# A streamed ReLU and row sum on one core: all loads but the first two blocks move to GpSimd's queue

## The chip, the core and the metric

The kernel runs on one core of one Trainium2 chip. The metric is the device time of one execution in microseconds (us), and smaller is better. A core has separate engines that run their own instruction streams and meet at semaphores: TensorE (PE, unused here), VectorE (DVE), ScalarE (ACT), GpSimd (POOL) and SyncE (SP). Data moves between HBM and the on-chip memory SBUF by 16 DMA engines, which take transfers from queues; an engine's instruction stream issues a transfer to a queue and goes on.

## The reference

```python
x = np.random.randn(32, 512, 1024).astype(np.float32)
relu_x = np.maximum(x, 0)
return np.sum(relu_x, axis=-1).astype(np.float32)
```

The input has 16,384 rows of 1,024 floats, 67.1 MB. Each row is clamped at zero and summed, which leaves 16,384 floats, 65.5 KB.

## The kernel before

The 16,384 rows are dealt out to the 128 partitions of SBUF, 128 rows to each, and worked on in eight blocks of 16 rows per partition. One block is [128 partitions, 16 rows, 1024 columns] of float32, 8.39 MB, and 64 KB in a row of SBUF. Three buffers, io0 to io2, are used in turn, so block j uses buffer j mod 3. The first block is a part of its own of the input; the other seven are cut from the rest. Either way the 16 rows of one partition lie next to each other in HBM, and a whole block moves as 128 packets of 65,536 bytes, eight on each of the 16 DMA engines.

The list `TWO` says how a block is computed. For the first three blocks ACT clamps the whole block in place (`clamp`, L120) and DVE then sums each row (`total`, L128). The fourth and fifth block do it in two halves, and the sixth in two parts of 7 rows with two further rows on ACT alone (`act_row`, L135, which clamps and sums one row). The seventh block is done row by row, nine rows by ACT and seven by DVE alone (`dve_row`, L143). The eighth block is the tail. It comes in shrinking loads of 8 rows, 4 rows, 2 rows and 280 columns, then the last row with the last 260 columns of the row before it, and at last two pieces of 240 and 244 columns of that row before it, which have small buffers of their own (piece0, piece1). Its rows are split between ACT and DVE too, and the last piece's sum is made on L227 from the piece and the partial sums beside it.

The helper `load` (L99) issues every load from SP, in order, on one hardware queue. Each load has its own semaphore, which reaches 16 when all 16 DMA engines have finished their share. From the fourth block on a load first waits on the semaphore `dve`, until DVE is done with the block that last used the buffer. Behind the 13 loads SP issues three stores (`store`, L110) of the row sums: the first block's 16 sums of each partition, then 110 sums, and the last 2. Then SP clears the semaphores (L46) and waits for the stores (L47).

`open_without_barrier` takes the opening barrier out and puts the first load (`EARLY = 1`) at the very start of SP's program. GpSimd does nothing but four small memsets of constants, which belong to the framework's opening. The order of all instructions is written out by hand; no scheduler moves them.

Of the kernel before, what the change touches and what calls it, by code (L numbers as in the profile page):

```python
# [9 lines left out]
ROWS = 16  # L10
NBUF = 3


TWO = [[16], [16], [16], [8, 8], [8, 8], [7, 7], []]
# [5 lines left out]
TAIL = [8, 4]  # L20
START_PIECE, END_PIECE = 280, 260
PIECES = [240, 244]

EARLY = 1


def kernel(tc: tile.TileContext, x: bass.AP, out: bass.AP):
    nc = tc.nc
    sems = Semaphores(tc)

    tc.close()
    tc.compile()
    nc.cur_bb = nc.bb_map[tc.start_bb_name]
    body = nc.cur_bb.bb.instructions
    ends = list(body)
    body.clear()
    n_stores = relu_sum(nc, sems, x, out)
    body.extend(ends)


    nc.cur_bb = nc.bb_map[tc.start_bb_name + "_end"]
    nc.cur_bb.bb.instructions.clear()
    nums = sorted(s.num for s in (*sems.loads, sems.act, sems.dve))
    cleared = range(nums[0], nums[-1] + 1)
    assert len(cleared) == len(nums)
    nc.sync.sem_clear(cleared)  # L46
    nc.sync.wait_ge(sems.stored, 16 * n_stores).then_inc(sems.stored, -16 * n_stores)  # L47
    open_without_barrier(tc, EARLY)


class Semaphores:
    def __init__(self, tc: tile.TileContext):
        n = len(TWO) + len(TAIL) + 2 + len(PIECES)
        self.loads = [tc.alloc_semaphore(f"load{i}") for i in range(n)]
        self.act = tc.alloc_semaphore("act")
        self.dve = tc.alloc_semaphore("dve")
        self.stored = tc.alloc_semaphore("stored")


def relu_sum(nc, sems: Semaphores, x: bass.AP, out: bass.AP):  # L60
# [24 lines left out]
    def rows(m, n):  # L85
        if m < ROWS:
            return xf[:, m : m + n, :]
        return xv[:, m - ROWS : m - ROWS + n, :]

    def sums(m, n):  # L90
        if m < ROWS:
            return of[:, m : m + n], res[:, m : m + n]
        return ov[:, m - ROWS : m - ROWS + n], res[:, m : m + n]

    n_load = n_act = n_dve = n_store = 0

    def load(dst, src, after=None):
        nonlocal n_load
        dma = nc.sync.dma_start(out=dst, in_=src)  # L99
        if after:  # L100
            dma.wait_op(sems.dve, after[1], "sem-ge")
        dma.then_inc(sems.loads[n_load], 16)
        n_load += 1
        return sems.loads[n_load - 1]

    def store(m, n, act, dve):
        nonlocal n_store
        dst, src = sums(m, n)
        nc.sync.wait_ge(sems.act, act)
        nc.sync.dma_start(out=dst, in_=src).wait_op(sems.dve, dve, "sem-ge").then_inc(  # L110
            sems.stored, 16
        )
        n_store += 1

    def clamp(ap, loaded):
        nonlocal n_act
        if n_act == 0:
            nc.scalar.preload_act_table(RELU).wait_op(loaded, 16, "sem-ge")  # L118
            loaded = None
        i = nc.scalar.activation(out=ap, in_=ap, func=RELU)  # L120
        if loaded is not None:
            i.wait_op(loaded, 16, "sem-ge")
        i.then_inc(sems.act, 1)
        n_act += 1

    def total(ap, m, n):
        nonlocal n_dve
        nc.vector.tensor_reduce(  # L128
            out=res[:, m : m + n], in_=ap, axis=mybir.AxisListType.X, op=ADD
        ).wait_op(sems.act, n_act, "sem-ge").then_inc(sems.dve, 1)  # L130
        n_dve += 1

    def act_row(ap, accum_out, loaded):
        nonlocal n_act
        i = nc.scalar.activation(out=ap, in_=ap, func=RELU, accum_out=accum_out)  # L135
        if loaded is not None:
            i.wait_op(loaded, 16, "sem-ge")
        i.then_inc(sems.act, 1)
        n_act += 1

    def dve_row(ap, accum_out, loaded):
        nonlocal n_dve
        i = nc.vector.tensor_scalar(  # L143
            out=ap,
            in0=ap,
            scalar1=0.0,
            scalar2=None,
            op0=MAX,
            op1=ADD,
            accum_out=accum_out,  # L150
        )
        if loaded is not None:
            i.wait_op(loaded, 16, "sem-ge")
        i.then_inc(sems.dve, 1)
        n_dve += 1

    freed = []
    m = 0
    for j in range(NB):
        buf = bufs[j % NBUF]  # L160
        loaded = load(buf[:, :, :], rows(m, ROWS), j >= NBUF and freed[j - NBUF])
        c = 0
        act_waits = dve_waits = loaded
        for n in TWO[j]:
            clamp(buf[:, c : c + n, :], act_waits)
            total(buf[:, c : c + n, :], m + c, n)
            act_waits = None
            c += n
        for _ in range(ACT[j]):
            act_row(buf[:, c, :], res[:, m + c : m + c + 1], act_waits)  # L170
            act_waits = None
            c += 1
        for _ in range(DVE[j]):
            dve_row(buf[:, c, :], res[:, m + c : m + c + 1], dve_waits)
            dve_waits = None
            c += 1
        assert c == ROWS
        freed.append((n_act, n_dve))
        m += ROWS


    buf = bufs[NB % NBUF]
    c = 0
    for n in TAIL:
        loaded = load(
            buf[:, c : c + n, :], rows(m, n), None if c else freed[NB - NBUF]
        )
        for i in range(n):
            if i % 2 == 0 or (n == 8 and i == 7):
                act_row(buf[:, c, :], res[:, m : m + 1], loaded if i == 0 else None)  # L190
            else:
                dve_row(buf[:, c, :], res[:, m : m + 1], loaded if i == 1 else None)
            c += 1
            m += 1

    flat = buf[:, :, :].rearrange("p c d -> p (c d)")
    src = rows(m, 4).rearrange("p c d -> p (c d)")
# [4 lines left out]
    last, w = parts[-1], PIECES[-1]  # L202
    others = [last[:, w + i : w + i + 1] for i in range(extra)]
    loaded = load(flat[:, at : at + b], src[:, :b])
    act_row(buf[:, c, :], res[:, m : m + 1], loaded)
    sums_act = n_act
# [3 lines left out]
    loaded = load(flat[:, at + end : at + 4 * D], src[:, end:])  # L210
# [13 lines left out]
    for i in range(len(PIECES) - 1):  # L224
# [3 lines left out]
        out=last[:, :],  # L228
# [6 lines left out]
    ).wait_op(sems.dve, n_dve, "sem-ge").then_inc(sems.dve, 1)  # L235
    n_dve += 1
    store(NT - 2, 2, n_act, n_dve)
    return n_store


def open_without_barrier(tc: tile.TileContext, n_loads: int):

    SP = mybir.EngineType.SP
    blocks = tc.nc.main_func.blocks
    opening = blocks[0].instructions
    body = next(b for b in blocks if b.name == tc.start_bb_name).instructions
    for i in list(opening):
        if isinstance(i, (mybir.InstDrain, mybir.InstEventSemaphore)):  # L250
            opening.remove(i)
    loads = [i for i in body if i.engine == SP][:n_loads]
    for i in loads:
        assert isinstance(i, mybir.InstDMACopy)
        body.remove(i)
    at = next(n for n, i in enumerate(opening) if i.engine == SP)
    opening[at:at] = loads
# [30 lines left out]
```

## Time and profile before

| what | value |
|---|---|
| time, median of 3 runs | 161.13 us (160.91 to 161.22) |
| span of the profiled execution, first to last instruction | 159.84 us |
| median time less that span (time around it) | 1.29 us |
| DVE busy | 117.6 us, 74% |
| ACT busy | 104.2 us, 65% |
| POOL busy | 0.2 us |
| DMA, mean over the span | 420 GB/s; packets take 97.9% of the 16 engines' span |
| HBM read | 67.11 MB |

The page gives an engine's busy time as a share of the span. A DMA packet is what one DMA engine moves at a stretch for one queue. "SPq" is the instruction stream of SP, which issues transfers and waits. A load's landing is the moment at which the last of its 16 semaphore increments arrives.

The trace also holds a start, a duration and a size for every packet, and the time of every semaphore increment. Where the text speaks of "the packet records" or "the landing records", it means these.

### The profile page before, as it was taken

How to read it: one execution, taken by the hardware profiler on the slowest of the kernel's cores; microseconds unless marked ns; L12 is line 12 of the kernel's file. 1: busy time of each engine (PE TensorE's matmuls, PEld its weight loads, DVE VectorE, ACT ScalarE, POOL GpSimd, SP SyncE). 2: the span in 40 equal slices, each digit the busy share in tenths (PEclk: the TensorE clock that was granted, in tenths of full speed). 3: DMA queues.
4: the chain of work that ended last, by engine and by line, in shares of the span. 5: the costliest groups of instructions: out<-in, count | busy, mean ns of one | idle time of the engine just before them, and what ended most of it. 6: DMA issues, size and time to landing. Idle time of an engine off the chain costs nothing.

```text
span 159.8 us, 120 instructions
## 1 busy us (share of the span) xinstructions
DVE 117.6 (74%) x43; ACT 104.2 (65%) x50; POOL 0.2 (0%) x4
## 2 busy tenths in 40 slices
DVE  0000000006999799994999999999999999999986
ACT  0000049993699808996099951999329993499994
POOL 0000000000000000000000000000000000000000
DMA  8996996996996997999989969969969969898993
GB/s 279 508 508 279 525 508 279 525 492 295 525 492 295 525 459 328 525 394 394 525 361 426 525 295 492 525 262 525 508 279 525 508 279 525 377 410 385 425 416 102
DMA packets 2304, 67.18 MB, mean 420 GB/s; under 512 B 640, under 2 KB 896, under 8 KB 1024
## 3 DMA queue, kind: packets, MB, share of 16 engines
q1 hardware_dynamic: 2304, 67.18, 97.9%
HBM read 67.11 MB, written 0.07 MB: 420 GB/s over the span
## 4 chain that ended last, share of the span: by engine, by line
DMA 44%; DVE 33%; ACT 17%; another core or an unknown queue 3%; SPq 1%; issue 0%
DMA io<-in_x_dram 44%; DVE res L128 32%; ACT io L120 17%; SPq L99 1%; DVE io L143 0%; DVE piece L227 0%; DVE piece L143 0%
## 5 line engine op out<-in xcount | busy, mean ns | idle before, releaser
L128 DVE TENSOR_REDUCE res<-io 128x8 f32<-128x8192 f32 (+2 forms) x9 | 101.1, 11286 | 40.2 <-ACT io L120 40.2
L120 ACT ACTIVATE io<-io 128x8192 f32<-128x8192 f32 (+2 forms) x9 | 81.7, 9111 | 26.0 <-DMA io<-in_x_dram 25.9
L135 ACT ACTIVATE io<-io 128x1024 f32<-128x1024 f32 x20 | 20.9, 1044 | 6.1 <-DMA io<-in_x_dram 6.1
L143 DVE TENSOR_SCALAR_CACHE_REDUCE io<-io 128x1024 f32<-128x1024 f32 (+2 forms) x15 | 15.8, 1110 | 0.6 <-DMA io<-in_x_dram 0.4
L118 ACT ACT_TABLE_LOAD x1 | 1.3, 1283 | 22.0 <-DMA io<-in_x_dram 22.0
L135 ACT ACTIVATION_READ_ACCUMULATOR io<-io 128x1 f32 x20 | 3.7, 187 | 0.0
L143 DVE DVE_READ_ACCUMULATOR io<-io 128x1 f32 x15 | 1.2, 82 | 0.0
L227 DVE TENSOR_SCALAR_CACHE_REDUCE piece<-piece 128x247 f32<-128x247 f32 x1 | 0.4, 410 | 0.0
L143 DVE TENSOR_SCALAR_CACHE_REDUCE piece<-piece 128x240 f32<-128x240 f32 x1 | 0.4, 398 | 0.0
L272 POOL MEMSET const-bfloat16-1.0<- 128x1 bf16 x1 | 0.1, 102 | 0.0
L272 POOL MEMSET const-uint8-127<- 128x1 uint8 x1 | 0.1, 102 | 0.0
L272 POOL MEMSET const-float32-1.0<- 128x1 f32 x1 | 0.1, 99 | 0.0
L272 POOL MEMSET const-float32-0.0<- 128x1 f32 x1 | 0.1, 98 | 0.2 <-issue 0.2
L143 DVE DVE_READ_ACCUMULATOR piece<-piece 128x1 f32 x1 | 0.1, 84 | 0.0
L227 DVE DVE_READ_ACCUMULATOR piece<-piece 128x1 f32 x1 | 0.1, 83 | 0.0
## 6 DMA issues: line engine op xcount, KB each, us to landing
io<-in_x_dram SPq DMA_DIRECT2D x1, 4096.0 KB, 21.6
io<-in_x_dram SPq DMA_DIRECT2D x1, 2048.0 KB, 26.1
io<-in_x_dram SPq DMA_DIRECT2D x1, 1164.0 KB, 28.4
io<-in_x_dram SPq DMA_DIRECT2D x1, 642.0 KB, 29.6
piece<-in_x_dram SPq DMA_DIRECT2D x1, 122.0 KB, 29.2
piece<-in_x_dram SPq DMA_DIRECT2D x1, 120.0 KB, 29.4
io<-in_x_dram SPq DMA_DIRECT2D x7, 26.9
out_dram<-res SPq DMA_DIRECT2D x1, 55.0 KB, 1.6
```

Of the source, the lines that this page charges most:

```text
L99: dma = nc.sync.dma_start(out=dst, in_=src)
L118: nc.scalar.preload_act_table(RELU).wait_op(loaded, 16, "sem-ge")
L120: i = nc.scalar.activation(out=ap, in_=ap, func=RELU)
L128: nc.vector.tensor_reduce(out=res[:, m : m + n], in_=ap, axis=mybir.AxisListType.X, op=ADD).wait_op(sems.act, n_act, "sem-ge").then_inc(se ...
L135: i = nc.scalar.activation(out=ap, in_=ap, func=RELU, accum_out=accum_out)
L143: i = nc.vector.tensor_scalar(out=ap, in0=ap, scalar1=0.0, scalar2=None, op0=MAX, op1=ADD, accum_out=accum_out,)
L227: nc.vector.tensor_scalar(out=last[:, :], in0=last[:, :], scalar1=0.0, scalar2=None, op0=MAX, op1=ADD, accum_out=res[:, NT - 2 : NT - 1],) ...
L272: nc = _bacc.Bacc("TRN2", target_bir_lowering=False, num_devices=1)
```

## The change

- A load whose number is 3 or more (`HARD = 3`), which is every load from the third block on, is issued by GpSimd instead of SP, with `single_packet=True`: all that one DMA engine moves for this load is to be one packet. There are 11 such loads. Those with a wait on `dve` keep it, on GpSimd.
- SP's second block becomes two loads, 14 rows and then 2 rows (`SHARE = 2`). ACT waits for both ahead of its clamp of that block. GpSimd waits for the landing of the 14 rows before it issues its first load.
- At the end GpSimd waits for `act`, for `dve` and for its 11 loads, resets its DMA state (`dma_reset`), clears its loads' semaphores and tells SP through a new semaphore `pool`. SP waits for that, and then clears the rest in two range clears instead of one.
- The computation, its split between ACT and DVE, the buffers and the three stores are the same.

```diff
+SHARE = 2
+HARD = 3
...
-    nc.sync.sem_clear(cleared)
+    nc.sync.wait_ge(sems.pool, 1)
+    nc.sync.sem_clear(span(*sems.hard))
+    nc.sync.sem_clear(span(sems.act, sems.dve, sems.pool))
...
+def span(*sems):
+    nums = sorted(s.num for s in sems)
+    assert nums[-1] - nums[0] + 1 == len(nums)
+    return range(nums[0], nums[-1] + 1)
...
-        n = len(TWO) + len(TAIL) + 2 + len(PIECES)
+        n = len(TWO) + 1 + len(TAIL) + 2 + len(PIECES)
+        self.soft, self.hard = self.loads[HARD:], self.loads[:HARD]
+        self.pool = tc.alloc_semaphore("pool")
...
     def load(dst, src, after=None):
         nonlocal n_load
-        dma = nc.sync.dma_start(out=dst, in_=src)
+        if n_load >= HARD:
+            if n_load == HARD:
+                nc.gpsimd.wait_ge(sems.loads[1], 16)
+            dma = nc.gpsimd.dma_start(out=dst, in_=src, single_packet=True)
+        else:
+            dma = nc.sync.dma_start(out=dst, in_=src)
...
-        loaded = load(buf[:, :, :], rows(m, ROWS), j >= NBUF and freed[j - NBUF])
+        if j == 1:
+            n = ROWS - SHARE
+            first = load(buf[:, :n, :], rows(m, n))
+            loaded = load(buf[:, n:, :], rows(m + n, SHARE))
+            nc.scalar.wait_ge(first, 16)
+        else:
+            loaded = load(buf[:, :, :], rows(m, ROWS), j >= NBUF and freed[j - NBUF])
...
     store(NT - 2, 2, n_act, n_dve)
+
+    nc.gpsimd.wait_ge(sems.act, n_act)
+    nc.gpsimd.wait_ge(sems.dve, n_dve)
+    for sem in sems.loads[HARD:n_load]:
+        nc.gpsimd.wait_ge(sem, 16)
+    nc.gpsimd.dma_reset(span(*sems.soft))
+    nc.gpsimd.sem_clear(span(*sems.soft))
+    nc.gpsimd.sem_inc(sems.pool, 1)
```

More of the change, by code (lines that the diff above doesn't have):

```diff
@@ L42 @@
     nc.cur_bb.bb.instructions.clear()
-    nums = sorted(s.num for s in (*sems.loads, sems.act, sems.dve))
-    cleared = range(nums[0], nums[-1] + 1)
-    assert len(cleared) == len(nums)
-    nc.sync.sem_clear(cleared)
+    nc.sync.wait_ge(sems.pool, 1)
+    nc.sync.sem_clear(span(*sems.hard))
+    nc.sync.sem_clear(span(sems.act, sems.dve, sems.pool))
     nc.sync.wait_ge(sems.stored, 16 * n_stores).then_inc(sems.stored, -16 * n_stores)
     open_without_barrier(tc, EARLY)
+def span(*sems):
+    nums = sorted(s.num for s in sems)
+    assert nums[-1] - nums[0] + 1 == len(nums)
+    return range(nums[0], nums[-1] + 1)
 class Semaphores:
     def __init__(self, tc: tile.TileContext):
-        n = len(TWO) + len(TAIL) + 2 + len(PIECES)
+        n = len(TWO) + 1 + len(TAIL) + 2 + len(PIECES)
         self.loads = [tc.alloc_semaphore(f"load{i}") for i in range(n)]
+        self.soft, self.hard = self.loads[HARD:], self.loads[:HARD]
         self.act = tc.alloc_semaphore("act")
         self.dve = tc.alloc_semaphore("dve")
+        self.pool = tc.alloc_semaphore("pool")
         self.stored = tc.alloc_semaphore("stored")
```

## The prediction

> **What bounds the kernel now.** I read the page first: the slices of the span, then the chain that ended last.
>
> ```profile
> DMA  8996996996996997999989969969969969898993
> q1 hardware_dynamic: 2304, 67.18, 97.9%
> DMA 44%; DVE 33%; ACT 17%; another core or an unknown queue 3%; SPq 1%; issue 0%
> ```
>
> The chain names DMA, DVE and ACT in turn, so it does not settle which is the limit. The DMA row is near full in every slice (its sixes are an effect of large packets being counted where they start). So I asked next for the busy time of each engine between the landings of the blocks.
>
> ```profile
> 22.05:41.37 19.32, 4.14 (x1) 15.14 (x3) 0.00 (x0) 1.00 1.00 434
> 41.37:60.72 19.35, 18.55 (x2) 13.86 (x2) 0.00 (x0) 1.00 1.00 434
> 60.72:80.06 19.34, 17.21 (x2) 13.85 (x1) 0.00 (x0) 1.00 1.00 434
> 80.06:99.42 19.36, 19.36 (x2) 13.95 (x2) 0.00 (x0) 1.00 1.00 433
> 99.42:118.76 19.34, 19.34 (x4) 13.95 (x2) 0.00 (x0) 1.00 1.00 434
> 138.12:157.17 19.05, 18.48 (x29) 18.00 (x34) 0.00 (x0) 1.00 0.98 413
> ```
>
> The columns are the stretch, its length, DVE, ACT and POOL, the clock, the DMA share and GB/s. A block lands every 19.34 us with the 16 DMA engines at a share of 1.00 and 434 GB/s. The transfers are the limit, without a pause from the first block to the tail; ACT has 5 us to spare in each block, and DVE, without a pause from 74.61 us, follows close behind. How close is read at the end, from the timeline.
>
> ```profile
> 154.08 1.04 ACT L135 ACTIVATE io<-io 128x1024 f32<-128x1024 f32 x1
> 155.53 1.06 ACT L135 ACTIVATE io<-io 128x1024 f32<-128x1024 f32 x1 [0.31 <-DMA io<-in_x_dram]
> 155.53 1.22 DVE L143 TENSOR_SCALAR_CACHE_REDUCE io<-io 128x1024 f32<-128x1024 f32 x1 [0.44 <-DMA io<-in_x_dram]
> 157.17 1.06 ACT L135 ACTIVATE io<-io 128x1024 f32<-128x1024 f32 x1 [0.49 <-DMA io<-in_x_dram]
> 157.96 0.41 DVE L227 TENSOR_SCALAR_CACHE_REDUCE piece<-piece 128x247 f32<-128x247 f32 x1
> ```
>
> Both engines wait for loads up to the end: ACT for 0.31 and 0.49 us, DVE for 0.44 us. A tail that lands up to about 0.5 us earlier is therefore followed by both; beyond that DVE, busy from 74.61 us on, would set the end itself.
>
> **How much the transfers can gain.** In the packet records a 65,536-byte packet is followed by the next after 2,414 ns, and a 32,768-byte one after 1,209. The difference, 1,205 ns for 32,768 bytes, is 27.2 bytes per ns and engine (435 GB/s on sixteen) and leaves about 4 ns for each packet. By that slope the packets of the tail cost 4 ns too much at 16,384 and 9,312 bytes, 9 at 5,136, 5 at 960 and 7 at 976. The 4-byte packet that tells a load's end costs 5 to 6 ns.
>
> *Removed.* Eleven loads become one packet per engine. The five blocks from the third to the seventh have 8 packets per engine each: 5 x 8 x 4.2 ns = 0.17 us. The six tail loads have 8 of each size: 8 x (4.4 + 4.4 + 4.5 + 9 + 5 + 7) ns = 0.27 us. The eleven 4-byte packets are 0.06 us. That is 0.50 us if everything goes, and 0.39 us if each load keeps the cost of one packet and its 4-byte packet stays. The other bound is zero: the trace has no packet of many rows, and the cost may belong to the row, not to the packet. The Trainium skill, "DMA: Bandwidth & Descriptors", section "Why small descriptors are slow (HBM only)", puts a fixed cost of about three cycles on each packet but calls packing worth it only at 256 bytes and less; by that the sum would be near zero here, where the records leave 0.39 to 0.50 us in forty-odd large packets and the tail. I take 0.50 us, by the meaning of one packet: it holds the load's rows and its end.
>
> *Added on the DMA engines.* The second block in two loads has eight more packets and one more 4-byte packet per engine: 0.04 us. The first store now stands behind no load on SP: it waits for the first block's sums, at 54.45 us, and goes out then. Before, its 64-byte packets (8 per engine, 7 ns apart) came after the last loads, from 156.59 us; now they cut into the stream for 0.06 us. Sum 0.10 us.
>
> *Moved to GpSimd, at no cost.* Five of the loads wait for DVE to free a buffer, on an engine that has nothing else to do than four memsets before 0.45 us.
>
> ```profile
> 37.23 17.22 DVE L128 TENSOR_REDUCE res<-io 128x16 f32<-128x16384 f32 x1 [37.23 <-ACT io L120]
> 55.26 17.22 DVE L128 TENSOR_REDUCE res<-io 128x16 f32<-128x16384 f32 x1 [0.81 <-ACT io L120]
> 126.22 1.77 SPq L99 DMA_DIRECT2D io<-in_x_dram  x4
> 128.04 0.94 SPq L99 DMA_DIRECT2D piece<-in_x_dram  x2
> ```
>
> The fourth block's buffer is free at 54.45 us and its transfer starts at about 60.0, when the third block's data are through: 5.5 us of cover. The fifth has 7 us (72.48 against 79.3), the sixth and seventh as much or more, and the first tail load 11 us (126.22 against 137.3). The six tail loads take SP 2.8 us to issue; even at the 2.7 us bound used below for each, the last is issued at 142.4, and its turn is at 156.6. If that cover were gone, each microsecond late would be one at the end. ACT's second wait for the second block costs nothing, since the 2 rows land last in any case.
>
> *Added at the end.* SP's range clear takes 58 ns at 158.8 us, and SP then waits until 159.80 for the last store. GpSimd's closing starts with DVE's end at 158.38: by the rows of a semaphore instruction (17 ns), of INC_SWDGE_SEM on POOL (27) and of the range clear (58), 13 waits, a reset and a clear are about 0.3 us, and SP's two clears 0.12. That is done by 158.9, beside the store. Free, while the reset takes less than about 0.9 us; beyond that it is paid in full, and I hold 0.5 us for that bound.
>
> *Added at the hand-over*, the only wait that decides. GpSimd's first load waits for the 14 rows. The 2 rows behind them are an eighth of a block, 2.42 us of transfer. The landing of the first block came 0.35 us after its last packet (22.03 against 21.69), so 2.1 us are left to wake GpSimd and start the third block. No row shows a load issued by POOL. The nearest rows are SP's: from issue to first packet 0.83 us for the last store and 1.01 us for the first load. From above I use the first load's whole time that is not a block's transfer, 22.05 - 19.34 = 2.7 us. At 2.7 the slowest DMA engine stands still for 0.6 us, and all behind it comes that much later; at 2.1 or less nothing is lost. I take 1.8, the middle: no cost. An earlier start is a gain nowhere, as the engines have work.
>
> **The sum.** -0.50 + 0.10 + 0 = -0.40 us. The span of 159.84 us becomes 159.44; with the 1.29 us between the span and the median of the runs shown that is 160.73 us, 0.25% less than 161.13. By a measurement that can tell about 0.2%, or 0.32 us, from no change, this is a small gain near the limit.
>
> **Rivals.**
> 1. *Nothing is saved* (the change does not do what it says): the cost belongs to each row, whether or not rows share a packet, or the 0.39 us are eaten by a small pause at the hand-over. 0.10 us more to 0.3 us less, about 161.1. For it: 4 ns is little, and the stream is already at 434 of 435 GB/s.
> 2. *The first GpSimd load is late* (slower). Place: the hand-over at 41 us. Price: 1 us for each microsecond beyond 2.1 us after the landing of the 14 rows, since the transfers have no pause later in which to catch up. It outweighs the saving from 2.5 us on, and is slower by over 0.2% from 2.8. At 3.3 us it is 161.13 - 0.40 + 1.2 = 161.9. For it: a queue not used before starts cold; the first packets of the execution took 3.1 to 3.4 us instead of 2.42.
> 3. *GpSimd's queue is slower.* Six of the eight blocks go through it, 6 x 19.34 = 116 us of transfer, so each per cent is 1.2 us. At 2% it is 163.0. For it: nothing in the profile; against it: the bytes and rows are the same, and 27.2 bytes per ns is the rate of every row size.
> 4. *The large packet overtakes.* If it starts while some engine still has part of the 2 rows to do, these and their end may wait 19.3 us behind it. ACT would start the second block at 60.7 instead of 41.4; DVE would free that block's buffer at 91.8 and the fifth block's transfer would start 12 to 13 us late: 174. The Trainium skill, "DMA: Bandwidth & Descriptors", section "Queues, rings and completion order", says that an engine changes queues in turn and only between packets, which speaks for this; no run here has two busy queues. Against it: the first packets' extra 0.7 to 1.0 us says that an engine reads that far ahead, so the last small rows are already under way from 1.3 us on, and 1.8 lies between 1.3 and 2.1.
> 5. *The closing shows*: the reset on GpSimd outlasts the last store by 0.5 us or more, 161.3 to 161.6.
>
> **How the numbers follow.** Forecast 0.46 (160.5 to 160.8); rival 1 0.20; rival 2 0.14; rival 3 0.08; rival 4 0.06; rival 5 0.06. Faster by over 0.2% is the forecast, 0.46; within 0.2% is rival 1, 0.20; slower is the rest, 0.34. The range runs from 160.3 (a saving of about 0.6 us, at which DVE sets the end, and 0.2 us for the spread of the runs, 160.91 to 161.22) to 162.4 (a start 3.8 us after the landing, or the closing's 0.5 us without a saving); outside lie rivals 3 and 4 and a corner of the others, under 0.2. The forecast's own range is 160.5 to 160.8.
>
> **What would show it.** Right: packets fall from 2304 to some 700; the blocks land about 19.31 us apart; the third block lands no later than 60.8 us; the last piece's sum starts near 157.5 instead of 157.96; SP's clears stand before the last landing. Wrong: packets as many as before (rival 1); the gap from the second landing to the third at 19.6 us or more (rival 2); 19.5 us and more between later landings (rival 3); ACT's second block after 60 us (rival 4); over 1.6 us from the last store's issue to the end (rival 5).

## The result, and the profile after

The changed kernel takes 163.19 us (163.06 to 163.94 in 4 runs) against 161.09 us (160.91 to 161.22) for the kernel before, a ratio of 1.0141 with a 95% interval of 1.0126 to 1.0156. It is 1.4% slower, and lies outside the range of the prediction. The profiled execution is the longest of the four: its span is 162.57 us, where before it was 159.84, so its trace has 2.7 us to account for, and the median 2.1.

First the DMA rows of the page of the changed kernel:

```profile
DMA  8997999996997998997997997996996997999981
DMA packets 2256, 67.18 MB, mean 413 GB/s; under 512 B 656, under 2 KB 656, under 8 KB 848
q0 software_dynamic: 1392, 50.33, 72.1%
q1 hardware_dynamic: 864, 16.84, 24.5%
```

q0 is GpSimd's queue: three quarters of the bytes now go through it. There are 2256 packets, not some 700, so the rows of 65,536 bytes have not been joined. Now the same stretches as before, from landing to landing (columns: stretch, its length, DVE, ACT and POOL, clock, DMA share, GB/s):

```profile
22.08:41.48 19.40, 4.22 (x1) 15.14 (x2) 0.67 (x1) 1.00 1.02 429
41.48:63.55 22.07, 21.18 (x2) 13.86 (x2) 0.53 (x1) 1.00 0.98 419
63.55:82.89 19.34, 14.49 (x2) 13.86 (x2) 0.53 (x1) 1.00 1.00 434
82.89:102.24 19.35, 19.35 (x2) 13.95 (x3) 0.53 (x1) 1.00 1.00 434
102.24:121.60 19.36, 19.36 (x4) 13.95 (x2) 0.53 (x1) 1.00 1.00 433
```

One stretch has changed. The third block, GpSimd's first, lands 22.07 us after the second instead of 19.35. All later blocks again come 19.34 to 19.36 us apart at 433 to 434 GB/s: GpSimd's queue is neither slower nor faster. What follows is the kernel before, shifted; ACT's and DVE's first work on the third block shows the shift. Before:

```profile
60.72 13.86 ACT L120 ACTIVATE io<-io 128x16384 f32<-128x16384 f32 x1 [5.49 <-DMA io<-in_x_dram]
74.61 66.64 DVE L128 TENSOR_REDUCE res<-io 128x16 f32<-128x16384 f32 x7 [2.13 <-ACT io L120]
```

and after the change:

```profile
39.30 0.67 POOL L111 DMA_DIRECT2D io<-in_x_dram  x1 [38.86 <-DMA io<-in_x_dram]
...
63.55 13.86 ACT L134 ACTIVATE io<-io 128x16384 f32<-128x16384 f32 x1 [8.21 <-DMA io<-in_x_dram]
...
77.44 66.64 DVE L142 TENSOR_REDUCE res<-io 128x16 f32<-128x16384 f32 x7 [4.85 <-ACT io L134]
...
160.71 0.41 DVE L247 TENSOR_SCALAR_CACHE_REDUCE piece<-piece 128x247 f32<-128x247 f32 x1
```

ACT waits 8.21 us for that block (5.49 before) and starts it at 63.55 (60.72), DVE starts at 77.44 (74.61), and the last piece's sum at 160.71 (157.96): 2.83, 2.83 and 2.75 us later. Nothing is lost or won behind the third block. The end costs nothing either: the last store is issued at 161.16 and seen at 162.57, 1.41 us as before, and SP's two range clears start at 161.54 and 161.62, beside it.

The packet records show what happens at the hand-over. They do not name their engine, so I joined each packet to the one that ends where it starts, which gives 16 sequences. Where an engine stands still, no end meets the next start; there each start was given the nearest end before it that was left. So in the first four lines of the table the two columns of times are measured, but which end goes with which start, and with it the length of each pause, is assumed. A "hard row" is a packet of SP's queue, q1. Six of the sixteen, in the changed kernel:

| last hard row ends | GpSimd's first row starts | standing still | that row takes |
|---|---|---|---|
| 40.34 us | 42.92 us | 2.58 us | 3.32 us |
| 40.38 | 42.52 | 2.15 | 3.20 |
| 40.40 | 41.58 | 1.18 | 2.84 |
| 40.48 | 40.91 | 0.43 | 3.00 |
| 40.69 | 40.70 | 0.00 | 3.06 |
| 41.08 | 41.11 | 0.03 | 3.26 |

The 14 rows landed at 39.00 and GpSimd issued at 39.30. The earliest of its rows starts at 40.68, the latest at 42.92. So every engine that was through before 40.68 stood still, and the two engines that start at 42.52 and 42.92 had run dry (had no packet left), since the last hard row of all ended at 41.08. On all sixteen the first row takes 2.8 to 3.3 us instead of 2.42, also on engines that did not stand still (the line at 40.69). The landing records show that few engines carry the loss: of the third block's 16 increments 14 come by 61.89 us, the other two at 63.01 and 63.53.

### The profile page after: what moved, and what is told of

It is laid out like the page before. It is cut to its first block, busy times and chain, and to the rows that moved or that the text cites. A ratio compares the mean times of both kernels' runs of the same rounds, so it can differ in the third digit from the quotient of the medians.

```text
span 162.6 us, 131 instructions
## 1 busy us (share of the span) xinstructions
DVE 117.6 (72%) x43; ACT 104.2 (64%) x50; POOL 6.1 (4%) x15
## 2 busy tenths in 40 slices
DMA packets 2256, 67.18 MB, mean 413 GB/s; under 512 B 656, under 2 KB 656, under 8 KB 848
## 4 chain that ended last, share of the span: by engine, by line
DMA 56%; DVE 33%; ACT 9%; POOL 1%; issue 0%; SPq 0%
DMA io<-in_x_dram 56%; DVE res L142 32%; ACT io L134 9%; DVE io L157 1%; POOL io L111 1%; DVE piece L247 0%; SPq L113 0%; DVE piece L157 0%
## 5 line engine op out<-in xcount | busy, mean ns | idle before, releaser
L111 POOL DMA_DIRECT2D io<-in_x_dram x9 | 4.9, 543 | 126.1 <-DVE res L142 87.2
L111 POOL DMA_DIRECT2D piece<-in_x_dram x2 | 1.1, 541 | 0.0
```

The costliest lines, as they stand in the source:

```text
L111: dma = nc.gpsimd.dma_start(out=dst, in_=src, single_packet=True)
```

## The experiments

Theory H, formed on this trace: the whole loss is the standstill at the hand-over, and GpSimd's queue is otherwise the same. Its rivals: the cut and the waits cost it (S), the joined packets do (P), or slower rows on GpSimd's queue (R), or a queue used for the first time is cold (C).

**The cut alone.** The kernel before, with

```diff
+        if j == 1:
+            n = ROWS - 2
+            first = load(buf[:, :n, :], rows(m, n))
+            loaded = load(buf[:, n:, :], rows(m + n, 2))
+            nc.scalar.wait_ge(first, 16)
...
```

> The kernel before with the second block cut into 14 and 2 rows alone; all loads stay on SP. Theory H (the whole loss of the change is the hand-over to GpSimd's first load): 161.1 to 161.2 us, since the cut costs eight more packets per engine, 0.04 us, and the third block lands at 60.7 to 60.8 us. Rival S (the cut and ACT's second wait cost the time): 162 us or more, with the second block landing later than 41.5 us.

161.20 us, 1.0009 times before (1.0000 to 1.0019); the third block's clamp starts at 60.74. S falls. The cut costs 0.18 us at the median, somewhat more than the 0.04 expected, at the limit of what the runs can tell.

**Without `single_packet`.**

```diff
-            dma = nc.gpsimd.dma_start(out=dst, in_=src, single_packet=True)
+            dma = nc.gpsimd.dma_start(out=dst, in_=src)
```

> The changed kernel without single_packet. Theory H: the rows of 65,536 bytes are packets of their own either way, so the time stays at 163.1 to 163.9 us, blocks land 19.34 us apart, and only the pieces' short rows come as more packets. Rival P (the joined packets hold the engines up or save something): the time moves by more than 0.3 us.

163.00 us, 1.0133 (1.0108 to 1.0158), as with it. The page's packet counts are the same, number for number:

```profile
DMA packets 2256, 67.18 MB, mean 415 GB/s; under 512 B 656, under 2 KB 656, under 8 KB 848
q0 software_dynamic: 1392, 50.33, 72.4%
```

The expectation was wrong in one point: the pieces' short rows stay joined too (eight rows of 960 bytes as 4,800 and 2,880). So that joining comes with GpSimd's queue, not with the flag, which changes no packet count here.

**One row of cover instead of two.**

```diff
-SHARE = 2
+SHARE = 1
```

> The changed kernel with 15 and 1 rows instead of 14 and 2, so that the cover of GpSimd's first load is 1.2 us instead of 2.4. Theory H: every DMA engine stands still 1.2 us longer at the hand-over, 164.3 us, with the third block landing at about 64.7 us. Rival R (the queue of GpSimd moves its rows more slowly, or the first store's packets slow it): 163.2 us, as the hand-over is not what costs.

162.99 us, 1.0124 (1.0109 to 1.0140).

```profile
62.61 13.86 ACT L134 ACTIVATE io<-io 128x16384 f32<-128x16384 f32 x1 [7.48 <-DMA io<-in_x_dram]
```

This breaks theory H in its first form, a fixed delay less a cover: 1.2 us less cover cost nothing more. Taken alone the run fits R, which gave 163.2; the next one decides. The records say what differs. Now all 16 engines stand still (the last hard row ends at 40.88, the first GpSimd row starts at 41.68), and they start 1.7 to 2.6 us after the landing of the 15 rows (40.00). With two rows the first started 1.7 us after the landing too, but the last 3.9, and 3.5 in the run without the flag. So 3.9 us is not a fixed time of GpSimd's load: starts that late were seen only where some engines had run dry while others still had hard rows.

**Four rows of cover.**

```diff
-SHARE = 2
+SHARE = 4
```

> The changed kernel with 12 and 4 rows, so that the cover is 4.8 us, more than the 3.9 us after which the last DMA engine started GpSimd's first load. Theory H without turns between the queues: the pause is gone, 161.1 us. Theory H with turns packet by packet: an engine that gets the new load early has 4 to 5 of the 8 small hard packets left, and each waits 2.4 us for a row of 65,536 bytes; the second block lands at 51 to 53 us instead of 41.5, DVE's chain is 7 to 9 us late, and the time is 167 to 170 us. Rival R: 163.2 us.

161.12 us, 1.0006 (0.9997 to 1.0016): the loss is gone. ACT's start of the second, third and fourth block:

```profile
43.79 13.86 ACT L134 ACTIVATE io<-io 128x16384 f32<-128x16384 f32 x1 [6.69 <-DMA io<-in_x_dram]
60.76 13.86 ACT L134 ACTIVATE io<-io 128x16384 f32<-128x16384 f32 x1 [3.12 <-DMA io<-in_x_dram]
80.08 13.95 ACT L134 ACTIVATE io<-io 128x8192 f32<-128x8192 f32 x2 [5.46 <-DMA io<-in_x_dram]
```

The third block comes at 60.76 (60.72 before). In the records no engine stands still; GpSimd's first row follows the last hard row at once and takes 2.42 us. The second block lands 2.4 us late, since on six engines the 4-byte packet that ends it comes after GpSimd's first row, but ACT has 5 us to spare there. So H holds for the place, R falls, and of the turns between the queues only that small packet shows, not the 7 to 9 us that the expectation feared.

**Three rows of cover**, run later:

```diff
-SHARE = 2
+SHARE = 3
```

> The changed kernel with 13 and 3 rows, a cover of 3.6 us between the 2.4 that did not suffice and the 4.8 that did. If the loss is the time by which the last engine starts after its hard rows are through (starts up to 3.9 us after the landing, 3.3 us of hard rows still to come from then on): only some engines stand still, for up to 0.6 us, and read their first row up to 0.7 us longer, so 161.2 to 162.3 us, varying between runs. If the loss has a fixed part that comes with any hand-over between the queues: 162.5 us or more.

161.14 us, 1.0006 (0.9997 to 1.0015).

```profile
41.39 13.86 ACT L134 ACTIVATE io<-io 128x16384 f32<-128x16384 f32 x1 [4.24 <-DMA io<-in_x_dram]
60.80 13.86 ACT L134 ACTIVATE io<-io 128x16384 f32<-128x16384 f32 x1 [5.56 <-DMA io<-in_x_dram]
```

Both blocks land as before, no engine stands still, and every first row takes 2.42 to 2.48 us. From two rows to three, all of the loss goes, not a part of it: there is no start at 3.9 us after the landing to be seen any more.

**A queue already used.** Theory C says that the first use is what costs.

```diff
...
+    warm = nc.alloc_sbuf_tensor("warm", [P, 16], F32)
+    nc.gpsimd.dma_start(out=warm[:, :], in_=rows(0, 1)[:, 0, :16], single_packet=True).then_inc(
+        sems.loads[-1], 16
+    )
...
```

> The changed kernel (14 and 2 rows) with one more small load, 64 bytes per partition into a buffer that nobody reads, issued by GpSimd at the very start. Theory C (a queue used for the first time starts cold): the first block from GpSimd starts on all engines within 2.1 us of the landing of the 14 rows, and the time is 161.1 to 161.6 us. Theory B (the engines are slow to take up a new load while they are full of hard rows): no change, 163.0 to 163.9 us, with the last engine starting 3.5 to 3.9 us after the landing.

163.03 us, 1.0144 (1.0086 to 1.0202); GpSimd's first rows start at 40.69 to 42.16, after a landing at 38.98. C falls. The last start, 3.2 us after the landing, is a little below the 3.5 to 3.9 given for the other theory.

**Six hand-overs to idle engines, on either queue.** GpSimd's, and SP's:

```diff
-            if n_load == HARD:
-                nc.gpsimd.wait_ge(sems.loads[1], 16)
+            if n_load <= HARD + 5:
+                nc.gpsimd.wait_ge(sems.loads[n_load - 1], 16)
```

> The changed kernel in which GpSimd's first six loads each wait for the whole landing of the load before, so that there are six hand-overs to idle engines. Theory B: each engine starts 1.7 to 2.6 us after the landing, as with one row of cover, the first row takes 0.7 us longer, and the last increment comes 0.35 us after the data: a hand-over costs about 3.2 us and the time is about 180 us. Theory C: the first costs 3 us or more and the others clearly less, 176 us or below. Theory A (two engines are late at every first packet of a load): 4.5 us or more each, 188 us.

```diff
+        if 2 <= n_load <= 7:
+            nc.sync.wait_ge(sems.loads[n_load - 1], 16)
         dma = nc.sync.dma_start(out=dst, in_=src)
```

> The kernel before in which SP's third to eighth load each wait for the whole landing of the load before: the same six hand-overs to idle engines, on SP's queue. From the first load of the execution, 2.7 us from issue to landing beyond the transfer, each costs about 2.75 us, and the time is about 177.5 us. Theory B then puts the price of GpSimd's queue beside SP's at about half a microsecond in each hand-over; if GpSimd's queue itself is slow, the difference is over 1.5 us in each.

180.78 us (1.1233, 1.1209 to 1.1257) and 176.43 us (1.0962, 1.0939 to 1.0986). ACT's starts on the second to fifth block, first with GpSimd's loads:

```profile
41.30 13.86 ACT L134 ACTIVATE io<-io 128x16384 f32<-128x16384 f32 x1 [4.24 <-DMA io<-in_x_dram]
63.90 13.86 ACT L134 ACTIVATE io<-io 128x16384 f32<-128x16384 f32 x1 [8.75 <-DMA io<-in_x_dram]
86.39 13.95 ACT L134 ACTIVATE io<-io 128x8192 f32<-128x8192 f32 x2 [8.63 <-DMA io<-in_x_dram]
109.18 13.95 ACT L134 ACTIVATE io<-io 128x8192 f32<-128x8192 f32 x2 [8.84 <-DMA io<-in_x_dram]
```

and with SP's:

```profile
41.12 13.86 ACT L122 ACTIVATE io<-io 128x16384 f32<-128x16384 f32 x1 [4.18 <-DMA io<-in_x_dram]
62.87 13.86 ACT L122 ACTIVATE io<-io 128x16384 f32<-128x16384 f32 x1 [7.89 <-DMA io<-in_x_dram]
84.78 13.95 ACT L122 ACTIVATE io<-io 128x8192 f32<-128x8192 f32 x2 [8.05 <-DMA io<-in_x_dram]
106.99 13.95 ACT L122 ACTIVATE io<-io 128x8192 f32<-128x8192 f32 x2 [8.26 <-DMA io<-in_x_dram]
```

A block comes 22.6 us after the one before from GpSimd ((109.18 - 41.30) / 3) and 22.0 us from SP, instead of 19.34: 3.3 and 2.6 us for each hand-over, the later ones much like the first, so C falls here too. A start from standstill is dear on both queues; GpSimd's own part is 0.7 us. In the records the first row starts 1.7 to 1.8 us after the landing from GpSimd and 1.0 from SP, the last of the 16 engines 0.5 to 1.1 us later, and most first rows of a block take 2.9 to 3.5 us, on both. With all engines idle, none starts as late as 3.9 us after the landing.

**A much earlier issue.** What holds the hand-over from being made safe by issuing much sooner:

```diff
-                nc.gpsimd.wait_ge(sems.loads[1], 16)
+                nc.gpsimd.wait_ge(sems.loads[0], 16)
```

> The changed kernel (14 and 2 rows) in which GpSimd's first load waits for the landing of the first block instead of the 14 rows, and so is issued at 22 us with 19 us of hard rows still to come. If the two queues take turns packet by packet once both are known to an engine: the second block lands at 56 to 61 us instead of 41.5, ACT and DVE start late, and the time is 172 to 178 us. If an engine finishes the hard rows that it already knows first, as the run with 4 rows of cover allows: the second block lands at 41.5 to 44 us, and the time is 161.1 to 161.4 us.

191.94 us, 1.1926 (1.1900 to 1.1952).

```profile
23.15 13.86 ACT L134 ACTIVATE io<-io 128x16384 f32<-128x16384 f32 x1
75.11 41.44 ACT L134 ACTIVATE io<-io 128x16384 f32<-128x16384 f32 x4 [38.10 <-DMA io<-in_x_dram]
128.61 13.95 ACT L134 ACTIVATE io<-io 128x8192 f32<-128x8192 f32 x2 [12.07 <-DMA io<-in_x_dram]
```

ACT waits 38.10 us for the second block. The records show the turns plainly: on one engine hard rows start at 23.12 and 25.24, GpSimd's at 27.35, a hard one at 29.77, GpSimd's at 31.88, and so on. The Trainium skill, "DMA: Bandwidth & Descriptors", section "Queues, rings and completion order", says that an engine goes round the queues packet by packet, and this run agrees; a turn is one row, 57,344 bytes from SP and 65,536 from GpSimd, although `single_packet` is set. The expectation had the mechanism and missed the size by 14 us: it forgot that the fourth block needs only the first buffer, so that it is issued at 54.57 and takes turns with the second block as well, which lands at 75.08 instead of 56 to 61.

**Four rows and a late first store.** The best version that the runs point to:

```diff
-SHARE = 2
+SHARE = 4
...
-    store(0, ROWS, *freed[0])
     store(ROWS, NT - ROWS - 2, sums_act, sums_dve)
+    store(0, ROWS, *freed[0])
```

> The changed kernel with 12 and 4 rows, and with the store of the first block's 16 sums issued behind that of the 110 sums, so that its 64-byte packets no longer cut into the loads. With the pause gone and the rows no faster, nothing is left but the eight more packets of the cut second block: 161.0 to 161.1 us, 0.06 us less than with the early store (161.12), and no version on GpSimd's queue is faster than the kernel before. If the rows were faster from GpSimd's queue after all, it would be 160.9 us or less.

161.11 us, 1.0006 (0.9997 to 1.0015). The store's 0.06 us cannot be seen, and no version on GpSimd's queue beats the kernel before.

**The same wait, on SP.** The cut of the first experiment, and

```diff
+        if n_load == 3:
+            nc.sync.wait_ge(sems.loads[1], 16)
         dma = nc.sync.dma_start(out=dst, in_=src)
```

> The cut into 14 and 2 rows with all loads on SP, where the third block's load waits for the landing of the 14 rows as GpSimd's first load does in the change. If the loss comes from how long GpSimd's first load takes to start on the last engine: from SP the engines start 1.0 to 1.9 us after the landing, as in the six hand-overs on SP's queue, which the 2.1 us of hard rows cover, and the time is 161.1 to 161.4 us. If any load that waits for the 14 rows costs as much: 162.5 us or more.

The median is 161.14 us, 1.0033 (0.9998 to 1.0067), but two of the ten runs took 163.0 and 163.2 us. In the profiled one, with a span of 160.0 us, no engine stands still, yet six of the 16 first rows take 2.45 to 2.81 us. So SP's start, 0.7 us sooner, just fits under two rows, without room to spare. That the two long runs were standstills fits, but they have no trace: not shown.

## Why the prediction was wrong

1. **The bound: right.** Transfers limit the kernel, and a delay at 41 us reached the end almost whole (2.83 us at the third block, 2.75 at the last sum).
2. **"Added at the hand-over ... I take 1.8, the middle: no cost": the step that failed**, worth 2.1 us at the median and 2.7 in the trace. Three things were wrong in it.
   - It measured the cover for the slowest engine (2.1 us) and left the engines that finish sooner out of the sum. But the fastest engines end their hard rows 0.7 us sooner, at 40.34, 1.34 us after the landing. The first start comes at 1.68 us, so they run dry, and one of the engines that ran dry comes back so late that it becomes the slowest: 42.92 + 3.32 = 46.24 us for the end of the first row, where the slowest engine without a pause would have been at 41.08 + 2.42 = 43.50. The difference, 2.74 us, is the loss of the trace: 1.84 of late start and 0.90 of a longer row.
   - It took one start time for all, and bounded it at 2.7 us. Sixteen engines start, from 1.68 to 3.92 us.
   - It had no term for the long first row, 2.8 to 3.3 us instead of 2.42. Rivals 2 and 4 cite the 3.1 to 3.4 us of the execution's first packets (13 of the 16 took so long, the other three 2.42 to 2.67), but no sum has a price for them.
3. **"Removed ... I take 0.50 us": wrong, about 0.** In the records a row of 65,536 bytes follows the one before after 2,414 ns at the median from either queue, with the flag or without. These rows stayed packets of their own, so rival 1's sign, as many packets as before, came true for them (the 48 packets fewer are the pieces' joined rows less the cut's added ones). What a large row would cost inside a joined packet no run here shows.
4. **"Added on the DMA engines", 0.10 us: right as far as the runs can tell.** With the pause gone, 161.12 against 161.02 is 0.10, but the interval (0.9997 to 1.0016) holds no change as well.
5. **Covers of the later loads, the end: right.** No later block waits, and the closing is hidden behind the last store.
6. **The rivals.** Rival 2 named the place and the sign; its price (1 us per microsecond after 2.1) gives 1.8 us for a start at 3.92 and misses the long first row. At 0.14 it had too little of the chance. Rival 3 is excluded by the later blocks, rival 5 by the end. Rival 4's mechanism exists, but here only in the run with the early issue, and as a 4-byte packet that is 2.4 us late with four rows of cover.

Left open: why the last starts come 3.2 to 3.9 us after the landing where some engines have run dry and others still work, and 2.2 to 2.9 us where all are idle (from GpSimd in both cases). A cold queue is excluded. Whether the engine that stops first starts last, and whether it is the same engine each time, can't be read from records that name no engine; nothing here shows what it waits for.

## What to carry to other kernels

Where the transfers are the limit, a hand-over between queues, or any load that waits for a landing, has to reach the *fastest* DMA engine before that one runs dry; measure the cover up to the end of the first engine's rows and not of the last, and add a margin, since a standstill costs far more than the gap (the gap was 0.34 us at the least, from 40.34 to 40.68, and the loss 2 us; with one more row of cover, 1.2 us, it was nothing). Do not make up for it by issuing much earlier, because two busy queues take turns row by row, and the load that is needed first then lands late. And before a flag is credited with a saving, look in the packet counts whether it changes anything: here they were 2256 with it and without.

## What the runs showed of the hardware

- A load on idle engines costs 2.6 us from SP and 3.3 us from GpSimd beyond its transfer, from landing to landing.
- GpSimd's issue holds its engine 0.53 us for one load (0.67 for the first), SP's 0.33 to 0.45.
- The rows move at the same pace from both queues, 2,414 ns at the median for 65,536 bytes on an engine.
- In the run with the early issue GpSimd's first row started 5.2 us after its issue at 22.14 on the engine shown, behind two further hard rows; in the changed kernel the first one started 1.4 us after its issue (39.30 to 40.68).
